# Layer 0's start and layer 1's start: eight conditioning pieces used whole, block 1's input made with block 0's, and the first four score maxima sent from ScalarE's queue

## The chip, the cores and the metric

The kernel runs on one core of a Trainium2 chip. The time is device microseconds (us) of one execution of the whole program; what is compared are medians of several executions. The engines of the core are TensorE (PE in the profile), VectorE (DVE), ScalarE (ACT), GpSimd (POOL) and SyncE (SP); each runs its own instruction list in order and waits on semaphores for the others. Nearly all DMAs are issued by SP.

## What is computed

A two-layer backbone in fp32 on 256 context and 2,048 latent tokens of width 1,024. Cut to what matters here:

```python
def ada_mod(cvec, w, b):                       # conditioning: silu(c) @ ada_w[l] + ada_b[l]
    m = jax.nn.silu(cvec) @ w + b
    shift, scale, gate = jnp.split(m, 3, axis=-1)
def modulate(x, mod, g):
    return rmsnorm(x, g) * (1 + scale) + shift
for l in range(DEPTH):                          # DEPTH = 2
    hp, hs = modulate(xp, mp, ...), modulate(xs, ms, ...)
    # l = 0: one projection of 1,824 columns -> latent attention (8 heads) || pooling, gates, output projection
    # l = 1: one projection -> windowed attention (16 heads, 4 KV heads, |i-j| <= 128, a sink logit per head), gate, output projection
    xp, xs = xp + mp[2] * rmsnorm(op, ...), xs + ms[2] * rmsnorm(os_, ...)
```

## The kernel before

**Precision.** Wide matmuls run on values split into two fp32r parts, high and low: ACT casts the value to fp32r (line 56), and DVE or POOL subtracts that from the value (line 57, the low part). A product is then three matmuls, high by high (line 113), low by high (114) and high by low (115).

**Start of layer 0.** The 2,304 tokens lie in nine blocks of 256 columns (block 0 is the context). The shift and scale of the modulation come from `ada_w` in 16 pieces of 128 x 1,024 values (512 KB), in the order j = 2, 0, 3, 1 of column groups and q = 0 to 3 within each; j = 2 and 0 serve the first four of eight row chunks of `h`, j = 3 and 1 the last four. Each piece is loaded (line 122), split, and multiplied by the conditioning vectors (lines 144, 145, 147). When a group is whole, ACT copies it out (L150), PE transposes it (L153), and DVE adds the bias and the low rows (L155, L156) and makes the scale (L160). `h_stats` loads a block of x, sums squares (ACT L179, POOL L180 to L185, PE L186, then L93 to L100) and multiplies x by the reciprocal root (L190; for block 0 on POOL). `h_mod` makes the high part on ACT (L199), the exact value on DVE (L200) and the low part on DVE (L201), four row chunks at a time. Block 1's `h` is made in the loop over blocks, when block 0 has done its second projection chunk. The projection's chunks 0 to 4 (`cr`, copied out by ACT at L457), the key's rotary part (`wkr`, L473 to L476) and chunks 9 to 12 follow in that order for each block. The weights of chunks 0 to 4 pass through a staging pool of twelve buffers, `ad`; those of `wkr`, chunks 9 to 12, `w_uk`, `w_uv` and `w_uq` through two staging buffers of the pool `p0`, so each load waits until the split of the load two before it is done.

**Start of layer 1.** Attention works in 18 units of 128 queries. Before a unit's scores, `approx1` multiplies its queries by the high part of the keys (L1107, L1115), DVE takes the maxima (L1110, L1116, L1121), and `max_b1` transposes them on PE (L1128), copies them on ACT (L1130) and writes them by DMA into row 64 of the unit's low queries (L1131). The scores' second matmul (L1164) reads that row. Keys lie in a ring that `load_piece` fills (L1043 to L1047). The first two units are looked ahead to during layer 1's last gate block, the following ones while earlier units run.

**Order.** The program is written in one order, and a scheduler orders each engine's list by a simulation of its own; so an edit in one place can move instructions in others. SP's list holds loads and stores alike; a store that waits for its data holds back what stands behind it.

Of the kernel before, what the change touches and what calls it, by code (L numbers as in the profile page):

```python
# [38 lines left out]
def hybrid_step(ctx: ExitStack, tc: tile.TileContext, I, O):  # L39
# [19 lines left out]
    def bank(tag, bufs):  # L59
        return psum.tile([128, 512], F32, tag=tag, name=tag, bufs=bufs)  # L60
# [73 lines left out]

    adaps = {}

    def ada_piece(l, j, q, wh, wl, ep):
        if q == 0:
            adaps[l, j] = bank("M", 3)
        ps = adaps[l, j]  # L140
        for i in range(2):
            k = 2 * q + i
            if k:
                pe.matmul(ps[0:2], lhsT=sch[:, k, 0:2], rhs=wl[:, i], start=False, stop=False)
            pe.matmul(ps[0:4], lhsT=sch[:, k], rhs=wh[:, i], start=k == 0, stop=k == KD - 1)
            if not k:
                pe.matmul(ps[0:2], lhsT=sch[:, k, 0:2], rhs=wl[:, i], start=False, stop=False)
        if q == 3:
            row = ep.tile([4, 512], F32, tag="adarow", name="adarow", bufs=1)
            act.copy(row, ps[0:4])  # L150
            pt = bank("M", 3)[:, 0:16].rearrange("p (m c) -> p m c", m=4)
            for m in range(4):
                pe.transpose(pt[:, m], row[:, 128 * m:128 * m + 128], ident[0:4, 0:4])  # L153
            ms = mods[l][:, 4 * j:4 * j + 4]
            dve.tensor_tensor(out=ms, in0=pt[:, :, 0:2], in1=adab[:, l, 4 * j:4 * j + 4].unsqueeze(2).to_broadcast([128, 4, 2]), op=ALU.add)  # L155
            dve.tensor_tensor(out=ms, in0=pt[:, :, 2:4], in1=ms, op=ALU.add)  # L156
            o = 4 * (j % 2)
            for c in range(2):
                if j in (2, 3):
                    dve.scalar_tensor_tensor(out=amod[l][:, o:o + 4, c], in0=ms[:, :, c], scalar=1.0, in1=npre[l][:, o:o + 4],  # L160
                                             op0=ALU.add, op1=ALU.mult)
                elif j in (4, 5):
                    dve.tensor_tensor(out=gmod[l][:, o:o + 4, c], in0=ms[:, :, c], in1=npost[l][:, o:o + 4], op=ALU.mult)
# [1 line left out]

    r_d = [dram.tile([128, T], F32, name=f"r{l}_d") for l in range(2)]

    def h_stats(hp, b, l, src, again, eng=None):
        cols = slice(256 * b, 256 * b + 256)
        x = hp.tile([128, KD, 256], F32, tag="xb", name="xb", bufs=1)  # L170
        sp.dma_start(out=x, in_=src[:, :, cols])
        if again:
            r = hp.tile([128, 256], F32, tag="rs_y256", name="rs_y", bufs=2)
            sp.dma_start(out=r, in_=r_d[l][:, cols])
        else:
            ss = bank("A", 1)[:, 0:256]
            for i in range(2):
                sq = hp.tile([128, 4, 256], F32, tag="sq", name="sq", bufs=box["sqb"])
                act.activation(out=sq, in_=x[:, 4 * i:4 * i + 4], func=AF.Square)  # L179
                pool.tensor_tensor(out=sq[:, 0:2], in0=sq[:, 0:2], in1=sq[:, 2:4], op=ALU.add)  # L180
                if i == 0:
                    s0 = hp.tile([128, 256], F32, tag="rs_t256", name="s0", bufs=1)
                    pool.tensor_tensor(out=s0, in0=sq[:, 0], in1=sq[:, 1], op=ALU.add)
            for i in range(2):
                pool.tensor_tensor(out=s0, in0=s0, in1=sq[:, i], op=ALU.add)  # L185
            pe.matmul(ss, lhsT=ones, rhs=s0, start=True, stop=True)  # L186
            r = rstd_of(hp, ss, [(0, 256, D)])
            sp.dma_start(out=r_d[l][:, cols], in_=r)
        for c in (slice(0, 4), slice(4, 8)):
            (eng or dve).tensor_tensor(out=x[:, c], in0=x[:, c], in1=r.unsqueeze(1).to_broadcast([128, 4, 256]), op=ALU.mult)  # L190
        return x

    def h_mod(hp, b, l, x):
# [163 lines left out]
    h0 = {}  # L357
    for i, (j, q) in enumerate([(j, q) for j in (2, 0, 3, 1) for q in range(4)]):
        if i == 4:
            h0[0] = h_stats(p0, 0, 0, xT, False, pool)  # L360
        ada_piece(0, j, q, *wload(ad, *wslot(p0, i % 9), ada_src(0, j, q), bufs=12), ad)


    w_in = {}
# [1 line left out]
    def w_in_load(c, s, eng=None, stg=p0, bufs=2):  # L366
        w_in[c] = wload(stg, *wslot(p0, s), W0[c], eng, bufs)

    for c in range(5):
        w_in_load(c, c, (dve, pool)[c % 2], ad, 12)  # L370
    h0[0] = h_mod(p0, 0, 0, h0[0])
    close_ad()
    lr, close_lr = open_pool("lr", "right")

# [73 lines left out]
    for b in range(NBL):  # L448
        h = h0.pop(b)
        t0 = 256 * b  # L450
        cols = slice(t0, t0 + 256)
        CS = None
        raw = lr.tile([128, 5, 256], F32, tag="cr", name="cr", bufs=1)
        for c in range(5):
            if b == 0 and c == 2:
                wkr_load()
            act.copy(raw[:, c], block_mm("S", w_in[c], h))  # L457
            if todo and c:
                todo.pop(0)()
            if c == 1 and b + 1 < NBL:  # L460
                h0[b + 1] = make_h(p0, b + 1, 0, xT)
        while todo:
            todo.pop(0)()
        if b == 2:
            ctx_part()
        if b:
            CS = lr.tile([128, 2, 256], F32, tag="CS", name="CS", bufs=1)
            for i in range(2):
                sp.dma_start(out=CS[:, i], in_=I["rope0"][i][:, t0 - SEQ:t0])
        ps = bank("S", 3)[0:64, 0:256]  # L470
        for k in range(KD):
            if k:
                pe.matmul(ps[0:32], lhsT=wkr[:, k - 1, 0:32], rhs=h[1][:, k - 1], start=False, stop=False)  # L473
            if k == KD - 1:
                pe.matmul(ps[0:32], lhsT=wkr[:, k, 0:32], rhs=h[1][:, k], start=False, stop=False)
            pe.matmul(ps, lhsT=wkr[:, k], rhs=h[0][:, k], start=k == 0, stop=k == KD - 1)  # L476
        e = p0.tile([128, 256], F32, tag="ev", name="ev", bufs=3)[0:32]
        act.copy(e, ps[32:64])
        dve.tensor_tensor(out=e, in0=ps[0:32], in1=e, op=ALU.add)
        if b == 0:  # L480
            sp.dma_start(out=O["state_krope"], in_=e)
        else:
            e = rope(lr, e, CS[0:32, 0], CS[0:32, 1], swap8)
        store_split(lr, e, kr_d, slice(0, 32), slice(kcol(t0), kcol(t0) + 256))
        c_hl = norm(b, raw)
        todo = lr_parts(b, c_hl, CS)
        for c in range(4):
            if b == 0:
                w_in_load(9 + c, 5 + c)
            spill(p0, block_mm("S", w_in[9 + c], h), vp_d[128 * c:128 * c + 128], cols)  # L490
            if b == 0:
                (lambda: lw_load("k", I["w_uk"]), lambda: lw_load("v", I["w_uv"]),
                 lambda: (lw_load("q0", I["w_uq"][0]), lw_load("q1", I["w_uq"][1])), lambda: lw_load("q2", I["w_uq"][2]))[c]()
# [630 lines left out]
    def max_b1(u):  # L1124
        t0 = UN1[u][0]
        mm = mxs.pop(u)
        pt = bank("M", 3)[0:16, 0:128]
        pe.transpose(pt, f(mm), ident)  # L1128
        ms = const.tile([16, 128], F32, tag="bms", name="bms", bufs=2)
        act.copy(ms, pt)  # L1130
        sp.dma_start(out=f(QV[u % NQ][1])[64:65], in_=ms)  # L1131
        es = const.tile([16, 128], F32, tag="bes", name="bes", bufs=2)
        act.activation(out=es, in_=pt, func=AF.Exp, scale=-SWA_SCALE, bias=sinkc)
        sp.dma_start(out=snk_d[:, t0:t0 + 128], in_=es)
# [87 lines left out]
        load_ctx()  # L1222

    def look_ahead(u):
        q1_to(u + 1)
        now1[0] = -22
        look1_to(8 * u + 8)
        max_b1(u)
        events1.clear()


    for b in range(NBL):
        next_h(NBL + b)
        h = h1.pop(NBL + b)
        for i, c in enumerate(range(8) if b < NBL - 1 else (5, 6, 0, 1, 2, 3, 4, 7)):
            if b == 0:
                w1_load(10 + c, c)
            spill(p1, block_mm(None if b < NBL - 1 else "S", w1[10 + c], h), g1_d[128 * c:128 * c + 128], slice(256 * b, 256 * b + 256), True)
            if i == 1 and b + 1 < NBL:
                next_h(NBL + b + 1)  # L1240
            if i == 3 and b + 1 == NBL:
                look_ahead(1)
        if b == 2:
            swa_start()
        if b == NBL - 2:
            ring["VLR"] = h1p.tile([128, 8, 256], F32R, tag="xb", name="VLR", bufs=1)
            load_piece(9)
            look_ahead(0)
    close_p1()
    tc.keep_in_program_order(act.preload_act_table_set("natural_log_exp_and_others"))  # L1250

# [21 lines left out]
    first = {}  # L1273
    for k, (u, g, i) in enumerate(seq1):
        first.setdefault(u, k)
    pace = ([-22] + [first[u] - 5 for u in range(NU1)], [0] + [8 * (u + 1) for u in range(NU1)])
    for p in range(8):
        at1(-21 if p < 3 else first[2 * p - 2] - 15, lambda p=p: load_piece(p))
    for m in range(NPRE):
# [127 lines left out]
```

## Time and profile before

| | |
|---|---|
| median of 3 executions | 3169.73 us (3160.95 to 3170.72) |
| profiled execution | 3158.63 us, span 3156.9 us |
| PE busy | 3008.6 us, 95% of the span |
| DVE, ACT, POOL busy | 70%, 56%, 50% |
| TensorE's mean granted clock | 0.981 of full speed |

The profile is of one execution, 11.1 us shorter than the median. Positions below are microseconds from the start of its span. "L145" is line 145 of the kernel before. A row of a timeline gives start, duration, engine, line, operation, output and inputs, shape and count, and in brackets the engine's idle time just ahead of it and what ended it.

### The profile page before, as it was taken

How to read it: one execution, taken by the hardware profiler on the slowest of the kernel's cores; microseconds unless marked ns; L12 is line 12 of the kernel's file. 1: busy time of each engine (PE TensorE's matmuls, PEld its weight loads, DVE VectorE, ACT ScalarE, POOL GpSimd, SP SyncE). 2: the span in 40 equal slices, each digit the busy share in tenths (PEclk: the TensorE clock that was granted, in tenths of full speed). 3: DMA queues.
4: the chain of work that ended last, by engine and by line, in shares of the span. 5: the costliest groups of instructions: out<-in, count | busy, mean ns of one | idle time of the engine just before them, and what ended most of it. 6: DMA issues, size and time to landing. Idle time of an engine off the chain costs nothing. (4 is left out here: it accounts for less than half of the span.)

```text
span 3156.9 us, 53087 instructions
## 1 busy us (share of the span) xinstructions
PE 3008.6 (95%) x19120; PEld 2587.7 (82%) x19120; DVE 2215.6 (70%) x3992; ACT 1777.0 (56%) x3579; POOL 1584.3 (50%) x1414
## 2 busy tenths in 40 slices
PE   6999999999999999999999999999997999989998
PEld 4999988897777777777679999999996776666998
DVE  6656657977888888888856656677324888767555
ACT  6444444436777777777774433333324877776433
POOL 3223232205777787777774534656002555455553
PEclk8999999999999999999999999999998999999999
DMA  6544468743202202212105554446527344441553
GB/s 237 157 137 133 149 193 257 244 129 90 55 19 56 61 16 58 56 42 65 57 12 177 169 188 150 138 129 190 151 94 153 83 105 102 99 98 50 164 171 118
DMA packets 379681, 375.09 MB, mean 119 GB/s; under 512 B 27904, under 2 KB 344952, under 8 KB 378264
## 3 DMA queue, kind: packets, MB, share of 16 engines
q1 hardware_dynamic: 379404, 371.68, 41.4%
q8 instruction: 150, 2.46, 0.3%
q14 instruction: 115, 0.94, 0.1%
q10 hardware_dynamic: 12, 0.00, 0.0%
HBM read 242.13 MB, written 129.24 MB: 118 GB/s over the span
## 5 line engine op out<-in xcount | busy, mean ns | idle before, releaser
L626 POOL TENSOR_TENSOR acc<-acc,ph 128x512 f32<-128x512 f32 x352 | 458.8, 1303 | 66.7 <-ACT ph L602 42.0
L602 ACT ACTIVATE ph<-S 128x512 fp32r<-128x512 f32 (+1 forms) x592 | 350.9, 593 | 195.1 <-PE S L600 186.9
L553 DVE TENSOR_REDUCE pm<-M 128x1 f32<-128x512 f32 (+1 forms) x656 | 392.1, 625 | 71.9 <-PE M L552 68.0
L614 DVE TENSOR_TENSOR pl<-S,ph 128x512 fp32r<-128x512 f32 (+1 forms) x496 | 334.8, 677 | 63.1 <-ACT S L607 55.4
L113 PE MATMUL S<-hh,wh 128*128 128x256 f32 x1296 | 370.1, 286 | 4.4 <-ACT wh L56 2.8
L114 PE MATMUL S<-hl,wh 128*128 128x256 f32 x1296 | 368.6, 285 | 4.1 <-DVE hl L201 4.1
L115 PE MATMUL S<-hh,wl 128*128 128x256 f32 x1296 | 368.5, 285 | 0.5 <-POOL wl L57 0.5
L607 ACT ACTIVATE S<-S 128x512 f32<-128x512 f32 (+1 forms) x496 | 291.7, 588 | 0.0
L113 PEld LDWEIGHTS S<-hh,wh 128*128 128x128 f32 x1296 | 249.4, 193 | 8.7 <-ACT wh L56 3.3
L114 PEld LDWEIGHTS S<-hl,wh 128*128 128x128 f32 x1296 | 249.7, 193 | 6.4 <-DVE hl L201 4.8
L115 PEld LDWEIGHTS S<-hh,wl 128*128 128x128 f32 x1296 | 249.4, 193 | 2.4 <-POOL wl L57 0.9
L598 PE MATMUL S<-QS,KHL 97*128 97x512 f32 (+1 forms) x592 | 236.6, 400 | 7.6 <-DVE pl L614 7.5
L599 PE MATMUL S<-QS,KHL 96*128 96x512 f32 (+1 forms) x592 | 235.3, 398 | 0.0
L600 PE MATMUL S<-QS,KHL 96*128 96x512 f32 (+1 forms) x592 | 233.0, 394 | 0.0
L552 PE MATMUL M<-KHL,QS 96*128 96x512 f32 (+1 forms) x656 | 227.0, 380 | 6.2 <-DVE pm L553 5.7
L639 PE MATMUL B<-pl,VV 128*65 128x512 f32 (+1 forms) x592 | 228.3, 396 | 1.2 <-DVE pl L614 1.0
L636 PE MATMUL A<-ph,VV 128*128 128x512 f32 (+1 forms) x592 | 215.0, 400 | 0.2 <-ACT ph L602 0.2
L1181 POOL TENSOR_TENSOR bpl<-bpf,bph 128x512 fp32r<-128x512 f32 x136 | 177.0, 1301 | 53.0 <-ACT bpf L1169 40.7
L113 PE MATMUL M<-hh,oh 128*128 128x256 f32 x696 | 197.1, 283 | 3.3 <-ACT oh L56 3.3
L114 PE MATMUL M<-hl,oh 128*128 128x256 f32 x696 | 195.5, 281 | 0.0
L115 PE MATMUL M<-hh,ol 128*128 128x256 f32 x696 | 195.3, 281 | 0.0
L1173 POOL TENSOR_SCALAR_AFFINE_SELECT bpf<-bpf 128x512 f32<-128x512 f32 x120 | 78.6, 655 | 203.8 <-ACT bpf L1169 189.6
(378 smaller groups left out, 9546.8 us busy)
## 6 DMA issues: line engine op xcount, KB each, us to landing
q_d<-ehl SPq DMA_DIRECT2D x126, 256.0 KB
stg<-in_ada_w SPq DMA_DIRECT2D x48, 512.0 KB
xb<-in_xT SPq DMA_DIRECT2D x18, 1024.0 KB
xb<-x_d SPq DMA_DIRECT2D x18, 1024.0 KB
stg<-in_w SPq DMA_DIRECT2D x35, 512.0 KB
hh<-q_d SPq DMA_DIRECT2D x24, 512.0 KB
kn_d<-ehl SPq DMA_DIRECT2D x40, 256.0 KB
v_d<-ve SPq DMA_DIRECT2D x20, 512.0 KB
```

Of the source, the lines that this page charges most:

```text
L113: pe.matmul(ps, lhsT=wh, rhs=xh, start=i == 0, stop=False)
L114: pe.matmul(ps, lhsT=wh, rhs=xl, start=False, stop=False)
L115: pe.matmul(ps, lhsT=wl, rhs=xh, start=False, stop=i == n - 1)
L553: dve.tensor_reduce(out=pms[u][:, s, i:i + 1], in_=ps[:, :w], axis=AX.X, op=ALU.max)
L598: pe.matmul(S[:, :n], lhsT=KH[s][0:97, kc], rhs=qh, start=True, stop=False)
L599: pe.matmul(S[:, :n], lhsT=KH[s][0:96, kc], rhs=ql[0:96], start=False, stop=False)
L600: pe.matmul(S[:, :n], lhsT=KL[s][0:96, kc], rhs=qh[0:96], start=False, stop=True)
L602: act.activation(out=ph[:, :n], in_=S[:, :n], func=AF.Exp, scale=MLA_SCALE)
L607: act.activation(out=pf[:, :n], in_=S[:, :n], func=AF.Exp, scale=MLA_SCALE)
L614: (pool if i in YS else dve).tensor_tensor(out=pl[:, :n], in0=pf[:, :n], in1=f(ph)[:, :n], op=ALU.subtract)
L626: pool.tensor_tensor(out=acc[:, :n], in0=acc[:, :n] if ph0 is None else f(ph0)[:, :n], in1=f(ph)[:, :n], op=ALU.add)
L639: pe.matmul(B[0:65, :n], lhsT=V[:, kts[i], 64:129], rhs=pl[:, :n], start=i == 0, stop=i == nk - 1)
```

## The change

- Pieces 0 to 7 of layer 0's conditioning (j = 2, 0) are handled as before. Pieces 8 to 15 (j = 3, 1) are not split: the fp32 piece goes into two fp32 matmuls with the fp32 conditioning vectors. Their result has two rows instead of four.
- Block 0's x by reciprocal root moves from POOL to DVE. The low parts of the first five projection weights are made by DVE, DVE, POOL, DVE, POOL (before DVE, POOL, DVE, POOL, DVE).
- Block 1's x is loaded ahead of the last two whole pieces, and its `h` is made right behind block 0's, ahead of the loop over blocks. The loop makes the next block's `h` from block 1 on.
- In layer 1 the DMA of the maxima (L1131) is issued by ACT for the first four units and by SP for the others. The look-aheads of units 0 and 1 are written into the last gate block at chunks 1, 2, 4 and 6, and the pacing table that interleaves later look-aheads starts accordingly.

```diff
     def ada_piece(l, j, q, wh, wl, ep, whole=None):
...
+        nr = 4 if whole is None else 2
         for i in range(2):
             k = 2 * q + i
+            if whole is not None:
+                pe.matmul(ps[0:2], lhsT=scf[:, k], rhs=whole[:, i], start=k == 0, stop=k == KD - 1)
+                continue
...
-            (eng or dve).tensor_tensor(out=x[:, c], in0=x[:, c], in1=r.unsqueeze(1).to_broadcast([128, 4, 256]), op=ALU.mult)
+            dve.tensor_tensor(out=x[:, c], in0=x[:, c], in1=r.unsqueeze(1).to_broadcast([128, 4, 256]), op=ALU.mult)
...
-        ada_piece(0, j, q, *wload(ad, *wslot(p0, i % 9), ada_src(0, j, q), bufs=12), ad)
+        if i < 8:
+            ada_piece(0, j, q, *wload(ad, *wslot(p0, 5 + i % 4), ada_src(0, j, q), bufs=12), ad)
+        else:
+            whole = ad.tile([128, 1024], F32, tag="stg", name="stg", bufs=12).rearrange("p (k m) -> p k m", k=2)
+            sp.dma_start(out=whole, in_=ada_src(0, j, q))
+            ada_piece(0, j, q, None, None, ad, whole)
...
-    for c in range(5):
-        w_in_load(c, c, (dve, pool)[c % 2], ad, 12)
+    for c in range(2):
+        w_in_load(c, c, dve, ad, 12)
+    h0[1] = h_stats(ad, 1, 0, xT, False)
     h0[0] = h_mod(p0, 0, 0, h0[0])
+    for c in range(2, 5):
+        w_in_load(c, c, (pool, dve)[c % 2], ad, 12)
+    h0[1] = h_mod(p0, 1, 0, h0[1])
...
-            if c == 1 and b + 1 < NBL:
+            if c == 1 and 0 < b < NBL - 1:
                 h0[b + 1] = make_h(p0, b + 1, 0, xT)
...
-        sp.dma_start(out=f(QV[u % NQ][1])[64:65], in_=ms)
+        (act if u < 4 else sp).dma_start(out=f(QV[u % NQ][1])[64:65], in_=ms)
...
     def look_ahead(u):
-        q1_to(u + 1)
         now1[0] = -22
         look1_to(8 * u + 8)
-        max_b1(u)
         events1.clear()
...
-            if i == 3 and b + 1 == NBL:
-                look_ahead(1)
+            if b + 1 == NBL:
+                {1: lambda: q1_to(2), 2: lambda: look_ahead(0), 4: lambda: (max_b1(0), look_ahead(1)),
+                 6: lambda: max_b1(1)}.get(i, lambda: None)()
...
-            look_ahead(0)
+            q1_to(1)
...
-    pace = ([-22] + [first[u] - 5 for u in range(NU1)], [0] + [8 * (u + 1) for u in range(NU1)])
+    pace = ([-6] + [first[u] - 5 for u in range(2, NU1)], [16] + [8 * (u + 1) for u in range(2, NU1)])
```

In the order that the scheduler makes, three places matter. **PE at the end of the conditioning** (`M` is the bank of a conditioning group or its transposes, `S` one of the projection, `sch` the split and `scf` the fp32 conditioning vectors, `stg` a loaded piece, `A` the bank of the row sums). Before, the last group's matmuls alternate with the first projection matmuls:

```order
L145 MATMUL M<-wh,sch 4x512
L113 MATMUL S<-hh,wh 128x256
L114 MATMUL S<-hl,wh 128x256
L144 MATMUL M<-wl,sch 2x512
L145 MATMUL M<-wh,sch 4x512
L144 MATMUL M<-wl,sch 2x512
L145 MATMUL M<-wh,sch 4x512
L113 MATMUL S<-hh,wh 128x256
L114 MATMUL S<-hl,wh 128x256
```

Now:

```order
L146 MATMUL M<-stg,scf 2x512 x8
L158 MATMUL M<-ident,adarow 128x2 x4
L146 MATMUL M<-stg,scf 2x512 x8
L192 MATMUL A<-s_305,ones 128x256
L113 MATMUL S<-hh,wh 128x256
L114 MATMUL S<-hl,wh 128x256
L115 MATMUL S<-hh,wl 128x256
```

Both whole groups and block 1's row sum stand ahead of the first projection matmul; the last group's transposes follow 14 projection matmuls later, and the matmuls of block 0's four later row chunks after those, in either kernel.

**DVE at block 0's later row chunks** (`wkr`, `kl`, `vl` and `wl` are low parts of weights). Before:

```order
L57 TENSOR_TENSOR wkr<-stg,wkr 128x8x32
L57 TENSOR_TENSOR kl<-stg,kh 128x1024
L200 TENSOR_SCALAR xb<-xb,amod_78,mod_76 128x256 x4
L201 TENSOR_TENSOR hl<-xb,hh 128x1024
L57 TENSOR_TENSOR wl<-stg,wh 128x1024
L57 TENSOR_TENSOR vl<-stg,vh 128x1024
```

Now:

```order
L100 SCALAR_TENSOR_TENSOR rs_y<-rs_t,rs_y 128x256
L207 TENSOR_TENSOR hl<-xb,hh 128x1024
L196 TENSOR_TENSOR xb<-xb,rs_y 128x1024 x2
L206 TENSOR_SCALAR xb<-xb,amod_78,mod_76 128x256 x4
L207 TENSOR_TENSOR hl<-xb,hh 128x1024
L206 TENSOR_SCALAR xb<-xb,amod_78,mod_76 128x256 x4
L207 TENSOR_TENSOR hl<-xb,hh 128x1024
L57 TENSOR_TENSOR wkr<-stg,wkr 128x8x32
L57 TENSOR_TENSOR kl<-stg,kh 128x1024
```

All of block 1's `h` stands between block 0's last low part and the split of `wkr`, which stood ahead of block 0's last low part before.

**ACT at the maxima of layer 1's third unit** (`bo` is an attention output, `bms` the maxima, `bes` the sink's term, `bph` the high part of the probabilities). Before:

```order
L1199 COPY bo<-A 65x512
L1199 COPY bo<-B 65x512
L1130 COPY bms<-M 16x128
L1133 ACTIVATE bes<-M,sinkc 16x128
L1167 ACTIVATE bph<-S 128x512
```

Now:

```order
L1214 COPY bo<-A 65x512
L1214 COPY bo<-B 65x512
L1145 COPY bms<-M 16x128
L1148 ACTIVATE bes<-M,sinkc 16x128
L1146 DMA hl<-bms 1x16x128
L1182 ACTIVATE bph<-S 128x512
```

The DMA has come to ACT's list two instructions behind the copy; in SP's list it stood behind two loads of KAR, a store and a load of KBR. PE's list from the first look-ahead matmul to the end of the third unit's scores is the same in both kernels, and the SP and PE lists of units 4 to 17 differ in the places of stores and look-aheads.

## Rows read from the trace of the kernel before

**Rows 1.** The page: the span, and its first part (busy time, share of the span, instructions by engine).

```profile
span 3156.9 us, 53087 instructions
PE 3008.6 (95%) x19120; PEld 2587.7 (82%) x19120; DVE 2215.6 (70%) x3992; ACT 1777.0 (56%) x3579; POOL 1584.3 (50%) x1414
```

**Rows 2.** Windows of the start: length, then busy time (and count) of each engine, granted clock, share of the 16 DMA engines, GB/s.

```profile
20.00:30.00 10.00, 7.23 (x28) 2.28 (x27) 9.74 (x12) 7.24 (x10) 3.73 (x3) 0.83 1.05 385
30.00:40.00 10.00, 4.69 (x21) 1.67 (x18) 9.90 (x15) 7.21 (x11) 7.02 (x3) 0.85 0.79 309
```

**Rows 3.** PE's timeline of the start: transposes of the second group, the waits, the last `wkr` matmul, and the first wait for block 1's `h`.

```profile
27.19 0.41 PE L153 MATMUL M<-ident,adarow 4*128 4x4 f32 x4 [1.62 <-ACT adarow L150]
...
38.61 0.58 PE L113 MATMUL S<-hh,wh 128*128 128x256 f32 x1 [2.77 <-ACT wh L56]
...
43.09 0.59 PE L144 MATMUL M<-wl,sch 128*2 128x512 f32 x1 [2.71 <-DVE wl L57]
...
56.32 0.58 PE L114 MATMUL S<-hl,wh 128*128 128x256 f32 x1 [2.69 <-DVE hl L201]
...
69.86 0.28 PE L476 MATMUL S<-hh,wkr 128*64 128x256 f32 x1
...
84.99 0.39 PE L114 MATMUL S<-hl,wh 128*128 128x256 f32 x1 [0.85 <-DVE hl L201]
```

**Rows 4.** PE's timeline: two neighbouring fp32r matmuls of 512 columns in the conditioning; and a row sum, which is an fp32 matmul of 256 columns (two records), with the fp32r matmuls of 256 columns behind it.

```profile
28.45 0.39 PE L144 MATMUL M<-wl,sch 128*2 128x512 f32 x1
28.68 0.40 PE L145 MATMUL M<-wh,sch 128*4 128x512 f32 x1
...
134.44 0.59 PE L186 MATMUL A<-s,ones 128*128 128x256 f32 x2
134.69 0.47 PE L113 MATMUL S<-hh,wh 128*128 128x256 f32 x1
134.99 0.28 PE L114 MATMUL S<-hl,wh 128*128 128x256 f32 x1
```

**Rows 5.** DVE's timeline: low parts of two pieces, exact values and a low part of `h`, two of a reciprocal root's steps, and x by reciprocal root (two instructions); and one such instruction on POOL.

```profile
30.17 4.53 DVE L57 TENSOR_TENSOR wl<-stg,wh 128x1024 fp32r<-128x1024 f32 x2
...
37.11 1.37 DVE L200 TENSOR_SCALAR xb<-xb,amod,mod 128x256 f32<-128x256 f32 x4
...
55.04 1.23 DVE L201 TENSOR_TENSOR hl<-xb,hh 128x1024 fp32r<-128x1024 f32 x1
...
77.33 0.43 DVE L98 SCALAR_TENSOR_TENSOR rs_t<-rs_y 128x256 f32<-128x256 f32 x1
...
78.25 0.87 DVE L100 SCALAR_TENSOR_TENSOR rs_y<-rs_t,rs_y 128x256 f32<-128x256 f32 x1
79.15 2.36 DVE L190 TENSOR_TENSOR xb<-xb,rs_y 128x1024 f32<-128x1024 f32 x2
...
30.34 3.28 POOL L190 TENSOR_TENSOR xb<-xb,rs_y 128x1024 f32<-128x1024 f32 x1 [6.45 <-DVE rs_y L100]
```

**Rows 6.** The way of chunk 10's and chunk 12's weights through the two staging buffers: their loads on SP, the cast of chunk 12's on ACT, and their low parts on DVE, between them the low part of `q0`, which frees chunk 12's buffer.

```profile
52.11 0.33 SPq L122 DMA_DIRECT2D stg<-in_w  x1
...
56.92 1.23 DVE L57 TENSOR_TENSOR wl<-stg,wh 128x1024 fp32r<-128x1024 f32 x1 [0.65 <-ACT wh L56]
...
66.65 1.49 DVE L57 TENSOR_TENSOR q0l<-stg,q0h 128x768 fp32r<-128x768 f32 x1
...
68.17 0.33 SPq L122 DMA_DIRECT2D stg<-in_w  x1
...
72.50 1.05 ACT L56 CAST wh<-stg 128x1024 fp32r<-128x1024 f32 x1 [0.21 <-DMA stg<-in_w]
...
73.58 1.43 DVE L57 TENSOR_TENSOR wl<-stg,wh 128x1024 fp32r<-128x1024 f32 x1 [1.35 <-ACT wh L56]
```

**Rows 7.** PE's timeline at the start of layer 1's attention: the last look-ahead matmul ahead of the third unit's scores, and those scores.

```profile
2432.12 0.57 PE L1107 MATMUL M<-KAR,hh 128*128 128x384 f32 x1
2440.90 1.22 PE L1164 MATMUL S<-hl,KBR 96*128 96x512 f32 x2 [8.22 <-DMA hl<-bms]
```

**Rows 8.** SP's timeline at the same place.

```profile
2431.13 0.79 SPq L1043 DMA_DIRECT2D KAR<-k_d  x1
...
2433.31 0.94 SPq L1045 DMA_DIRECT2D KBR<-k_d  x1
2434.36 0.62 SPq L1131 DMA_DIRECT2D hl<-bms  x1
```

**Rows 9.** ACT's timeline there: the maxima's copy and the sink's term.

```profile
2428.00 0.26 ACT L1130 COPY bms<-M 16x128 f32<-16x128 f32 x1 [0.44 <-PE M L1128]
2428.17 0.35 ACT L1133 ACTIVATE bes<-M,sinkc 16x128 f32<-16x128 f32 x1
```

**Rows 10.** Windows around it, columns as in rows 2.

```profile
2425.00:2450.00 25.00, 15.25 (x55) 11.11 (x54) 13.96 (x42) 6.97 (x14) 4.71 (x5) 0.66 0.74 151
2450.00:2475.00 25.00, 25.00 (x122) 18.62 (x121) 18.24 (x49) 20.69 (x41) 14.58 (x14) 1.00 0.41 87
```

**Rows 11.** The page's third part: DMA queues, with packets, MB and share of 16 engines.

```profile
q1 hardware_dynamic: 379404, 371.68, 41.4%
...
q10 hardware_dynamic: 12, 0.00, 0.0%
```

**Rows 12.** A query of line 571, where layer 0's attention issues its first two units' maxima from ACT (duration min/median/max in ns, then first and last start).

```profile
L571 ACTq DMA_DIRECT2D QS<-ms x2: 608/896/1184, 706.1 to 707.4; - x2
```

More of the change, by code (lines that the diff above doesn't have):

```diff
@@ L135, in hybrid_step, with ada_piece @@
     adaps = {}
-    def ada_piece(l, j, q, wh, wl, ep):
+    def ada_piece(l, j, q, wh, wl, ep, whole=None):
         if q == 0:
@@ L148, in ada_piece @@
         if q == 3:
-            row = ep.tile([4, 512], F32, tag="adarow", name="adarow", bufs=1)
-            act.copy(row, ps[0:4])
-            pt = bank("M", 3)[:, 0:16].rearrange("p (m c) -> p m c", m=4)
+            row = ep.tile([4, 512], F32, tag="adarow", name="adarow", bufs=1)[0:nr]
+            act.copy(row, ps[0:nr])
+            pt = bank("M", 3)[:, 0:4 * nr].rearrange("p (m c) -> p m c", m=4)
             for m in range(4):
-                pe.transpose(pt[:, m], row[:, 128 * m:128 * m + 128], ident[0:4, 0:4])
+                pe.transpose(pt[:, m], row[:, 128 * m:128 * m + 128], ident[0:nr, 0:nr])
             ms = mods[l][:, 4 * j:4 * j + 4]
             dve.tensor_tensor(out=ms, in0=pt[:, :, 0:2], in1=adab[:, l, 4 * j:4 * j + 4].unsqueeze(2).to_broadcast([128, 4, 2]), op=ALU.add)
-            dve.tensor_tensor(out=ms, in0=pt[:, :, 2:4], in1=ms, op=ALU.add)
+            if nr == 4:
+                dve.tensor_tensor(out=ms, in0=pt[:, :, 2:4], in1=ms, op=ALU.add)
             o = 4 * (j % 2)
@@ L166, in hybrid_step, with h_stats @@
     r_d = [dram.tile([128, T], F32, name=f"r{l}_d") for l in range(2)]
-    def h_stats(hp, b, l, src, again, eng=None):
+    def h_stats(hp, b, l, src, again):
         cols = slice(256 * b, 256 * b + 256)
@@ L359, in hybrid_step @@
         if i == 4:
-            h0[0] = h_stats(p0, 0, 0, xT, False, pool)
-        ada_piece(0, j, q, *wload(ad, *wslot(p0, i % 9), ada_src(0, j, q), bufs=12), ad)
+            h0[0] = h_stats(p0, 0, 0, xT, False)
+        if i < 8:
[4 more added lines that the diff above has]
+            ada_piece(0, j, q, None, None, ad, whole)
     w_in = {}
```

## The prediction

> **What bounds the kernel now.** I read the page first: PE is busy 3,008.6 of 3,156.9 us [rows 1]. At most 148 us can be had without removing PE work, and an edit that shortens work on another engine counts only where PE waits for it. So I looked for PE's waits at the two places of the change.
>
> At the start, DVE is the bound from 20 to 40 us: it is busy 9.74 and 9.90 of each 10 us, while PE has 7.23 and 4.69 [rows 2]. PE waits four times there: for a copy at 27.2, for a cast at 38.6, for a low part of a piece at 43.1, and for block 0's second low part, which lets it go at 56.32 [rows 3]. From there it runs with short waits; one is 0.85 us at 85 for block 1's `h` [rows 3]. The DMA engines are full from 20 to 30 us at 385 GB/s [rows 2]: a 512 KB piece takes 1.36 us.
>
> At the start of layer 1's attention PE ends its look-ahead at about 2432.7 and waits 8.22 us for the third unit's maxima [rows 7]. They were ready for the DMA at 2428.5, behind the copy and the sink's term on ACT [rows 9], but SP issued it at 2434.36, behind the stores and the loads of KAR and KBR in its list [rows 8].
>
> **Whole pieces.** Eight casts, eight low parts and 32 matmuls go. A low part is 1.23 us [rows 6], or 2.3 while POOL multiplies x [rows 5], so DVE is rid of some 10 to 18 us before 48 us. In their place stand 16 fp32 matmuls of 512 columns. The trace has fp32 matmuls of 256 columns: from 134.44 to 134.99, less 0.12 for the fp32r matmul between, is 0.43 us, 3.6 times the fp32r one [rows 4]. For 512 columns I take twice that, 0.86 us. A piece then costs PE 1.72 us, where four fp32r matmuls at 0.23 [rows 4] cost 0.92, and this is more than the 1.36 us of its load: in this stretch PE becomes the bound in DVE's place.
>
> PE is free at 27.5, after the second group's transposes [rows 3]. Group j = 3: 8 x 0.86 = 6.9, to 34.4. Copy and transposes, some 1.1 (0.41 [rows 3] and the copy ahead), to 35.5. Group j = 1: to 42.4. Its last piece, with block 1's 1 MB ahead of it, lands at about 35 by the pace of the queue, so loads hide. Then the row sum 0.43 and 14 first-half projection matmuls at 0.12, and the transposes: 44.9. From there DVE's list (the second place of the order) is: the bias 0.2, a low part 1.23, the three steps of block 1's root 0.43 + 0.43 + 0.87, four exact values 1.37, and the low part 1.23 [rows 5, 6]; 5.8, so block 0's second half is ready at 50.6. Before it was 56.3 [rows 5]: **5.7 us earlier**. x by reciprocal root on DVE, 2.36 for two against 3.28 for one on POOL [rows 5], is ahead of this, where DVE now has time, and costs nothing.
>
> **Block 1's h made early.** It puts 2.36 + 2 x 1.37 + 2 x 1.23 = 7.6 us of DVE work [rows 5] between block 0's last low part and the split of `wkr`: that split ends at 50.6 + 7.6 + 0.4 = 58.6. PE has 34 second-half matmuls and two more projection chunks to do until about 62, so it does not wait for `wkr` itself. What is queued behind it does: the two staging buffers. Chunk 10's load needs the buffer of `wkr`, and from issue to the end of the low part it took 52.11 to 58.15, 6.0 us [rows 6]. So chunk 10 is ready at 64.6, chunk 11 at 70.6. In the other buffer `w_uk` is split at 59.8, `w_uv` at 65.8 and `q0` at 71.5; chunk 12's load starts then, and its cast ended 5.4 us after the issue [rows 6]: 76.9. Before, chunk 12 was ready at 75.0 [rows 6] and PE came to it only at about 80.5 (69.86 + 0.2 [rows 3], three chunks of 24 x 0.12, 1.8 for three row sums at 0.43 and a short wait). So of 5.7 us **3.6 are left** at chunk 12, and 2.1 turn into a wait for its weights. The 0.85 us at 85 go [rows 3], since block 1's `h` is long ready. The start's term is **-4.5 us**: bounds 0, if each of the four loads in the chain takes 1 us longer, and -6.6, if none of it binds (5.7 + 0.85).
>
> **The maxima from ACT's queue.** ACT issues the DMA at 2428.5 instead of SP at 2434.36 [rows 8, 9]; the issue takes ACT 0.6 to 1.2 us by the two such DMAs of layer 0 [rows 12], and ACT has nothing to do there until PE's scores come. When does it land? PE resumed 6.5 us after SP's issue [rows 7, 8], with three key loads ahead in the queue. The page counts ACT's DMAs as a queue of their own: q10 has 12 packets against q1's 379,404 [rows 11]. If that queue does not stand behind the key loads, which are issued later anyway (2431.13 on [rows 8]), the row lands before 2432.7 and the wait goes: **-8.2 us**. If it takes 6.5 us all the same, it lands at 2435.0 and 2.3 us of wait stay: -5.9. I take -8.2, since what the DMA stood behind was issued after 2431. Above that, the granted clock is 0.66 in the window with the wait and 1.00 in the next [rows 10]; without the wait some of the work at half clock may be done at full: up to 2 us more.
>
> A rule speaks against it: the Trainium skill, "DMA: Bandwidth & Descriptors", section "Issuing engines are not separate DMA queues", says that DMAs of all issuing engines run on the same 16 DMA engines and interleave, and that several issuers save only the time of issuing. By it the term would be the 5.9 us of issue alone. The rows agree with its first half (one set of 16 engines, full in the start), and no row here shows a landing of q10 beside a full q1.
>
> **The look-aheads spread out.** PE's list is the same from the first look-ahead to the end of the third unit's scores, so this moves nothing there: 0. In later units stores and look-aheads change places in SP's and PE's lists; the trace has no row for that, and I bound it by the waits of this place, half of 8.2 each way: -4 to +4, taken as 0.
>
> **Sum.** -4.5 - 8.2 = -12.7 us. The profiled execution took 3,158.6 with a span of 3,156.9: it would be 3,145.9. The median of the runs is 3,169.7, 11.1 above it; with the same difference the forecast is **3,157.0 us**.
>
> **Rivals.**
> - *The DMA lands late all the same*, 6.5 us after its issue. For it: the 16 engines are busy 0.74 of that window [rows 10]. Against: the separate queue and the later key loads. Term -5.9, total -10.4: 3,159.3. Chance 0.13. (The rule of the Trainium skill above would give this case.)
> - *The start gives nothing*: the chain of two staging buffers takes 1 us more per load, or PE runs the fp32 matmuls at half clock, where 16 of them take 27.5 us instead of 13.8 (the granted clock was 0.83 and 0.85 with PE half idle [rows 2]; now PE is full, which speaks against). In the first case the term is 0, total -8.2: 3,161.5; in the second block 0 is ready at 64.4, 8 us later than before, and the total is about 0: 3,169. Chance 0.2 and 0.04.
> - *Slower*: from the fifth unit on the maxima still go by SP. If a moved store, which waits for ACT's copy, stands ahead of them or of a unit's queries, PE waits there as it did for the third unit, 8.2 us each time [rows 7]. One such wait leaves -4.5, two are +3.7 (3,173), and from the second on the change loses. For it: SP's list is not the same in units 4 to 17. Against: stores stood ahead of the later maxima before too, and the trace has no second wait of that size for them. Chance 0.07.
> - *It does more*: nothing binds in the chain and the clock adds 2 us: -16.8, 3,152.9. Chance 0.1.
>
> **How the numbers follow.** The forecast has 0.46. A measurement of this kernel can tell about 0.3%, 9.5 us, from no change. The forecast, the late landing and the larger gain lie beyond that bound or at it, the empty start within it; with the +-4 us of the later units I get 0.56 faster, 0.36 the same, 0.08 slower. The range runs from the larger gain with 4 us of later units and some spread of the runs (3,146) to the case of an empty start with 8 us on top (3,169).
>
> **What would show it.** In the changed kernel's trace: the fp32 matmuls back to back from about 27 to 42 us with DVE no longer full; PE released for block 0's second half near 50.6; a wait of about 2 us near 75 on a cast of chunk 12's weights; no wait on block 1's `h`; a wait below 2 us ahead of the third unit's scores. The forecast is wrong if the fp32 matmuls cost over 1 us each, if PE waits over 5 us for weights between 60 and 80, if the maxima's wait stays, or if a wait over 4 us appears in units 4 to 17.

## The result

| | before | after |
|---|---|---|
| median of 6 executions each | 3166.09 us | 3182.34 us (3176.38 to 3190.6) |
| ratio | 1 | 1.0055 [1.0037, 1.0073] |
| profiled execution, span | 3156.9 us [rows 1] | 3174.6 us |

The changed kernel is slower by 0.55%, some 16 to 17 us, outside the predicted range. Two marks on PE cut both profiled executions into three stretches: the third unit's first scores, and the first output projection that waits for its weights. (Units are numbered from 0 below: the third unit is unit 2.)

| stretch | before | after | difference |
|---|---|---|---|
| start to third unit's scores | 2440.90 [rows 7] | 2439.87 | -1.0 |
| to the output projection | 498.84 | 523.45 | **+24.6** |
| to the end of the span | 217.2 | 211.3 | -5.9 |
| sum | 3156.9 | 3174.6 | +17.7 |

The ends of the second stretch are the first rows below; it will be called the **middle stretch**. It repeats well: 498.2 to 500.3 in seven kernels, the one before and six of those below (`layer1_only`, `whole_only`, `after_keep`, `before_keep`, `start_keep`, `whole_keep`). The other two move by several us between executions of equal work (the last is 211 to 217 in all profiles, and from the row at 183 below to the third unit's scores it is 2,251 to 2,266), so only the middle one is read to the microsecond. Within this spread the first stretch shows only 1.0 us of the 7.3 that the start (4.25) and the third unit's shorter wait (3.1) gained. The third unit's wait is 5.14 us now (8.22 [rows 7]). PE's timeline of the changed kernel, and the projection's row of the kernel before behind it:

```profile
2439.87 1.22 PE L1179 MATMUL S<-hl,KBR 96*128 96x512 f32 x2 [5.14 <-DMA hl<-bms]
...
2963.32 0.57 PE L113 MATMUL M<-hh,oh 128*128 128x256 f32 x1 [3.75 <-ACT oh L56]
```

```profile
2939.74 0.58 PE L113 MATMUL M<-hh,oh 128*128 128x256 f32 x1 [3.34 <-ACT oh L56]
```

**The start** came out near what was worked out (how much of that is luck is said further down). PE's timeline of the changed kernel:

```profile
26.59 7.03 PE L146 MATMUL M<-stg,scf 128*2 128x512 f32 x16
34.33 0.41 PE L158 MATMUL M<-ident,adarow 2*128 2x2 f32 x4 [0.72 <-ACT adarow L155]
34.67 7.03 PE L146 MATMUL M<-stg,scf 128*2 128x512 f32 x16
...
52.16 0.58 PE L114 MATMUL S<-hl,wh 128*128 128x256 f32 x1 [4.65 <-DVE hl L207]
...
72.49 0.70 PE L410 MATMUL B<-sq,ones 128*128 128x256 f32 x2 [2.01 <-POOL sq L106]
...
79.35 0.39 PE L113 MATMUL S<-hh,wh 128*128 128x256 f32 x1 [2.09 <-ACT wh L56]
...
183.03 0.63 PE L113 MATMUL M<-ch,kh 128*128 128x256 f32 x3 [2.06 <-ACT ch L56]
```

Each group's eight fp32 matmuls (two records each) take 7.03 us back to back. Block 0's second half goes on at 52.16 (56.32 [rows 3]), chunk 12 waits 2.09 us for its cast, and no wait for block 1's `h` is left. The row at 183.03 stands in the kernel before at 187.28. In windows, DVE is no longer full, and PE nearly is from 30 us on (before: [rows 2]):

```profile
20.00:30.00 10.00, 7.79 (x26) 2.10 (x25) 7.06 (x10) 2.48 (x6) 3.70 (x3) 0.95 1.06 374
30.00:40.00 10.00, 9.28 (x26) 2.02 (x25) 6.51 (x13) 6.73 (x9) 6.25 (x5) 1.00 1.04 402
```

**The middle stretch.** PE's waits from 2455 to 2950 us, first of the kernel before, then of the changed one (engine, bank, line, what is waited for: us in total, times, longest):

```profile
PE M L1107 <- DMA mix0h<-q_d: 6.6, 3, 2.7
PE A L1195 <- DVE bpl L1181: 4.1, 8, 1.0
PE M L1107 <- DMA hh<-q_d: 4.0, 3, 2.2
PE B L1195 <- DVE bpl L1181: 3.5, 6, 0.7
...
PE A L1195 <- POOL bpl L1181: 1.4, 1, 1.4
...
PE B L1195 <- POOL bpl L1181: 0.4, 1, 0.4
```

```profile
PE M L1122 <- DMA hh<-q_d: 12.9, 7, 2.9
PE B L1210 <- DVE bpl L1196: 7.4, 12, 0.9
PE M L1122 <- DMA mix0h<-q_d: 5.8, 3, 3.0
PE A L1210 <- DVE bpl L1196: 2.2, 5, 0.8
PE A L1210 <- POOL bpl L1196: 1.9, 1, 1.9
...
PE B L1210 <- POOL bpl L1196: 1.1, 2, 0.9
```

`q_d` holds the queries (`hh` and `mix0h` are buffers for their high part), `bpl` is the low part of the probabilities. The look-aheads meet queries that have not landed ten times, 18.7 us in all, where it was six times and 10.6. One of them, with SP's row of the load and PE's of the wait, in the changed kernel:

```profile
2554.09 0.60 SPq L1100 DMA_DIRECT2D hh<-q_d  x1
...
2562.86 0.58 PE L1122 MATMUL M<-KAR,hh 128*128 128x384 f32 x2 [2.91 <-DMA hh<-q_d]
```

There are three query buffers, so unit u's load is issued when unit u-3 has done its scores. The load landed 8.8 us after its issue; PE came to the look-ahead after 5.9. How far a look-ahead stands behind that point is in PE's list, which the scheduler makes. Counted in score steps (a step is the score matmuls of one unit, one group of heads and one tile of keys; 328 in all; 499 us over 328 is 1.5 us each), for units 6 to 17:

```
before       17 14 10  5  5  6  6  4  2  3  3  4
after        10  5  4  2  5  3  4  2  3  2  4  3
```

8.8 us are six steps: eleven of the changed kernel's twelve look-aheads stand below that (ten wait), seven of the kernel before's (six wait); unit 8, with 4 steps, is the wait in the rows above. The text says below how much of the 24.6 us this accounts for.

### The profile page after: what moved, and what is told of

Read it like the earlier page. It is cut to its first block, busy times and chain, and to the rows that moved or that the text cites. A ratio compares the mean times of both kernels' runs of the same rounds, so it can differ in the third digit from the quotient of the medians.

```text
span 3174.6 us, 53061 instructions
## 1 busy us (share of the span) xinstructions
PE 3017.9 (95%) x19120; PEld 2586.4 (81%) x19120; DVE 2202.6 (69%) x3984; ACT 1769.5 (56%) x3571; POOL 1577.0 (50%) x1412
## 3 DMA queue, kind: packets, MB, share of 16 engines
q1 hardware_dynamic: 379276, 371.65, 41.2%
```

## The experiments

The theories. **A**: the edit of the start shifts the scheduler's simulated times; that moves the later look-aheads ahead of their queries, and the middle stretch gets longer. **B**: the loss is of layer 1's own edits (ACT's queue, spreading). **C**: the query waits only replace others; the loss is elsewhere. For the third unit's maxima, **D**: they land late behind the loads, whatever queue issues them; **E**: SP's issue time sets the wait.

### The start alone, layer 1 alone

`start_only` is the changed kernel with layer 1's three edits taken back; `layer1_only` has these and the start of before.

```diff
-        (act if u < 4 else sp).dma_start(out=f(QV[u % NQ][1])[64:65], in_=ms)
+        sp.dma_start(out=f(QV[u % NQ][1])[64:65], in_=ms)
...
-    pace = ([-6] + [first[u] - 5 for u in range(2, NU1)], [16] + [8 * (u + 1) for u in range(2, NU1)])
+    pace = ([-22] + [first[u] - 5 for u in range(NU1)], [0] + [8 * (u + 1) for u in range(NU1)])
```

> The whole edit of the start, with layer 1's code as before. Theory A (the start's edit shifts the scheduler's simulated times, and by that the places of layer 1's look-aheads in PE's list: unit 7's maxima stand 20 score steps ahead of its first score instead of 10, so that PE meets the look-ahead while the queries are still being loaded): the loss stays, about 1.005 of before or a little more, about 17 to 22 us slower, with some 19 us of PE waits for query loads in units 4 to 17 (before 10.6). Theory B (layer 1's own edits, the DMA from ACT's queue and the pacing, cost it): the start's 5 us are kept, 0.998 of before.

> The edits of layer 1 alone (DMA of the first four maxima from ACT, look-aheads spread out, pacing), with the start as before. Theory A: PE's list in layer 1 is that of before, so only the third unit's wait changes, from 8.2 to about 5 us: 3 us faster, 0.999. Theory B: 15 to 20 us slower, 1.005 to 1.006.

`start_only`: 1.0041 [1.0026, 1.0056], 3176.99 us, some 13 us slower where A expected 17 to 22. Its look-aheads stand as in the changed kernel, its middle stretch is 517.6 us, and its query waits are the same (18.6 us):

```profile
PE M L1122 <- DMA hh<-q_d: 13.0, 7, 2.8
...
PE M L1122 <- DMA mix0h<-q_d: 5.7, 3, 3.0
```

`layer1_only`: 0.9992 [0.9979, 1.0005], 3160.01 us; the look-aheads of units 4 to 17 stand as before, middle stretch 500.3, third unit's wait 5.7. Its query waits are longer than those of the kernel before (12.3 us, six times), at no cost to the stretch:

```profile
PE M L1107 <- DMA mix0h<-q_d: 6.7, 3, 2.5
PE M L1107 <- DMA hh<-q_d: 5.6, 3, 2.4
```

So 18.8 of the 24.6 us come with the start's edit, 2,400 us ahead of where they are paid. Layer 1's edits alone bring 1.4. B falls as the main cause; the 5.8 us between `start_only` and the changed kernel, with the same look-aheads and query waits in both, are not explained.

### The two halves of the start's edit

`whole_only`: whole pieces, but block 1's `h` in the loop as before. `early_h_only`: all 16 pieces split, block 1's `h` early. Layer 1 as before in both.

```diff
-    h0[1] = h_stats(ad, 1, 0, xT, False)
...
-    h0[1] = h_mod(p0, 1, 0, h0[1])
...
-            if c == 1 and 0 < b < NBL - 1:
+            if c == 1 and b + 1 < NBL:
```

```diff
-        if i < 8:
-            ada_piece(0, j, q, *wload(ad, *wslot(p0, 5 + i % 4), ada_src(0, j, q), bufs=12), ad)
-        else:
...
+        ada_piece(0, j, q, *wload(ad, *wslot(p0, i % 9), ada_src(0, j, q), bufs=12), ad)
```

> The start with whole pieces 8 to 15, x by reciprocal root on DVE and the new split of the weights' low parts, but block 1's h made in the loop over blocks as before; layer 1's code as before. Theory A: here the look-aheads of units 5 to 8 stand only 4 steps ahead of their units, the query loads have long landed, and layer 1's attention is not slower than before; with 2 to 5 us from the start about 0.997 to 0.999 of before. Theory B has no layer-1 edit to blame here either and gives the start's gain alone, 0.998 to 0.999; it differs from A in the waits for query loads, which by B stay at 10.6 us.

> Block 1's h made with block 0's, with all 16 pieces split as before (x by reciprocal root on DVE); layer 1's code as before. Theory A: the look-aheads stand nearly where they do in the changed kernel, so layer 1 loses 12 to 20 us of it again; the start itself does not gain, since DVE gets more work where it is full: 1.005 to 1.008 of before. Theory B: only the start's loss, 1 to 5 us, 1.000 to 1.0015.

`whole_only`: 1.0004 [0.9991, 1.0018], 3167.43 us: not the small gain that A gave it, though the middle stretch is 499.6 and the query waits 6.5 us. Where that gain went is not shown. `early_h_only`: 1.0077 [1.0057, 1.0097], 3192.16 us, middle stretch 520.1; DVE stays full there (10.00 of 10 us from 30 to 40) and PE waits 5.21 us at 41.04 and 4.85 at 60.43. The lists, as above:

```
whole_only   16 16 16 16 15 12 14 10  5  2  3  3
early_h_only 10  5  2  4  5  2  5  2  3  2  4  3
```

The order is not a matter of more or less work at the start: with one half most look-aheads stand further behind than before, with the other as close as with both. That the start's edit reaches the order through the scheduler's simulated times, as A says, is argued; the runs show the edit and the order.

### The order held

One line per look-ahead keeps its first matmul where the program writes it, from unit 3 on. `after_keep` is the changed kernel with it, `before_keep` the kernel before.

```diff
-                    pe.matmul(ps[:, b:b + w], lhsT=qa[:, h], rhs=KAR[:, g, a:a + w], start=x == 0, stop=x == len(runs) - 1)
+                    mmi = pe.matmul(ps[:, b:b + w], lhsT=qa[:, h], rhs=KAR[:, g, a:a + w], start=x == 0, stop=x == len(runs) - 1)
+                    if u >= 3 and hp == 0 and g == 0 and h == h0 and x == 0:
+                        tc.keep_in_program_order(mmi)
```

> The changed kernel with one thing added: the first look-ahead matmul of each unit from the fourth on is kept at its place in the written order, so that no unit's look-ahead starts more than 21 score steps ahead of the unit's first score (in the changed kernel up to 36). Theory A (the look-aheads ran into the query loads): the waits for query loads in units 4 to 17 fall from 18.7 to under 4 us, layer 1 loses nothing any more, and the time is 12 to 20 us below the changed kernel's, about 0.998 to 1.000 of before. Theory C (in that order it is not the queries: PE waits for DVE, ACT and POOL there, or the clock falls for other reasons): the query waits move to others, and the time stays at 1.004 to 1.006.

> The kernel before with the same hold on the look-aheads. Theory A: its 10.6 us of waits for query loads fall to under 4, 4 to 8 us faster than before, 0.997 to 0.999. Theory C: no change or slower, since PE has less to fill its other waits with, 1.000 to 1.002.

Both have 19 steps for each of the units 6 to 17, and no wait for queries. `after_keep`: **0.9983 [0.9974, 0.9992]**, 3157.23 us, middle stretch 500.3; that is some 23 us below the changed kernel, where A expected 12 to 20. `before_keep`: 0.9995 [0.9982, 1.0008], 3162.95 us, middle stretch 499.6. PE's waits in the stretch, `after_keep`, then `before_keep`:

```profile
PE A L1212 <- DVE bpl L1198: 10.3, 18, 1.4
...
PE B L1212 <- DVE bpl L1198: 2.5, 7, 0.7
```

```profile
PE A L1197 <- DVE bpl L1183: 11.5, 18, 2.4
PE A L1195 <- ACT bph L1181: 4.1, 2, 3.5
...
PE B L1197 <- DVE bpl L1183: 2.0, 4, 0.7
```

The same edit takes 23 us out of the middle stretch of one kernel and leaves the other as it was. A forecast 4 to 8 us for `before_keep`; they didn't come: its 10.6 us of query waits were replaced by waits for the probabilities' low part on DVE (13.5 us, before 7.6) and for their high part on ACT (4.1, before none). That much of C holds: removing query waits is not worth their sum.

### The loss made in the kernel before

`before_far` is `before_keep` with the look-aheads paced to be done 21 steps ahead of a unit's scores, not 5; `after_near` is `after_keep` with 2 steps. Paced earlier, a look-ahead stands closer behind its queries' load.

```diff
-    pace = ([-22] + [first[u] - 5 for u in range(NU1)], [0] + [8 * (u + 1) for u in range(NU1)])
+    pace = ([-22] + [first[u] - (5 if u < 4 else 21) for u in range(NU1)], [0] + [8 * (u + 1) for u in range(NU1)])
```

```diff
-    pace = ([-6] + [first[u] - 5 for u in range(2, NU1)], [16] + [8 * (u + 1) for u in range(2, NU1)])
+    pace = ([-6] + [first[u] - (5 if u < 4 else 2) for u in range(2, NU1)], [16] + [8 * (u + 1) for u in range(2, NU1)])
```

> The kernel before, nothing of the change in it, with the look-aheads paced 16 score steps earlier from the fifth unit on and their first matmuls held there. That gives PE the list that the changed kernel has: units 6 to 9 have their maxima at score steps 57, 72, 89 and 112 (changed kernel 62, 77, 92, 112; before 69, 86, 102, 117). Theory A: this order alone makes the loss, 12 to 20 us slower than before, 1.004 to 1.006, with 17 to 20 us of waits for query loads in units 4 to 17. If the loss needs anything else of the change (the start's loads, ACT's queue), it is 1.000 to 1.001.

> after_keep with the look-aheads paced 3 steps later still (they start 18 steps ahead of their unit's first score instead of 21, and the maxima are done 3 steps ahead instead of 5). Theory A has nothing to gain there, since no query is waited for any more; if the maxima now come too late, their DMA is waited for in more units: 0 to 6 us slower than after_keep.

```
before_far    5  3  4  3  5  3  4  3  4  5  3  4
after_near   22 22 22 22 22 22 22 22 22 22 23 23
```

`before_far`: 1.0083 [1.0063, 1.0103], 3194.6 us, middle stretch 523.9, as in the changed kernel, with nothing changed at the start; the whole loses more than the 1.004 to 1.006 expected. Its query waits:

```profile
PE M L1107 <- DMA hh<-q_d: 11.2, 7, 2.6
PE M L1107 <- DMA mix0h<-q_d: 10.3, 4, 3.5
```

`after_near`: 1.002 [1.0009, 1.0032], 3169.61 us, middle stretch 507.6, some 12 us slower than `after_keep` where at most 6 were expected. Too late costs as well: now the scores wait for maxima.

```profile
PE S L1181 <- DMA hl<-bms: 5.4, 2, 4.2
```

### What the parts are worth in a good order

`start_keep` and `whole_keep` are `start_only` and `whole_only` with the held order (the edit of `after_keep`).

> The start's edit with layer 1's code as before and the hold on the look-aheads: after_keep without the DMA from ACT's queue and without the spreading. The third unit's wait should be 8.2 to 8.5 us instead of 4.9: 2 to 4 us slower than after_keep, about 0.999 to 0.9995 of before. If the queue is worth nothing in the end (what PE gains there it waits for DVE a little later), it equals after_keep, 0.998.

> As start_keep, but block 1's h is made in the loop over blocks as before; so the start's gain is that of the whole pieces alone. If the early h is worth its 0.85 us and no more, this equals start_keep within 1 us; by the prediction's chain (the early h holds back the staging buffers and costs 2.1 us of wait at chunk 12) it is 1 to 2 us faster than start_keep.

`start_keep`: 0.9981 [0.9969, 0.9993], 3159.49 us. I had expected it 2 to 4 us slower than `after_keep`, for want of ACT's queue; it is equal within the intervals, so **the queue and the spreading are worth nothing that can be measured** (each interval is 3 to 4 us wide either way), though the third unit's wait is 8.3 us here and 4.9 in `after_keep`. `whole_keep`: 0.9984 [0.9973, 0.9995], 3161.25 us; against `start_keep`, the early `h` cannot be told from nothing either. That it is 2 parts in a thousand below `whole_only`, with a middle stretch only 1.4 us shorter (498.2), is not explained. Against `before_keep` the start's edit gives 1.4 parts in a thousand, 4.4 us; the intervals of the two overlap.

### The maxima without the large loads ahead of them

In `after_keep_hold` and `before_keep_hold` the loads of unit 4's queries and of the fourth piece of keys wait for the third unit's maxima: ACT first writes the maxima into the buffers that these loads fill. They are `after_keep` and `before_keep` otherwise.

```diff
+        if u == 4:
+            for z in (qa[0:16, 0], qa[64:80, 0], qb[0:16, 0]):
+                act.copy(z, ms2[0])
...
+        if p == 3:
+            for z in (KAR[0:16, 0, a:a + 128], KAR[64:80, 0, a:a + 128], KBR[0:16, 0, a:a + 128]):
+                act.copy(z, ms2[0])
```

> The changed kernel with both holds, so the maxima go by ACT's queue with nothing ahead on the DMA engines. By D the wait is under 2 us as with SP's queue, and the queue makes no difference (the changed kernel's 5.1 us with ACT's queue was the same landing time behind the same loads). With the start's 5 us kept this is the best of the four, about 0.996 of before, 3,150 to 3,155 us. By E the changed kernel's wait would have fallen to under 2 already, so E cannot explain its 5.1 us.

> As before_keep, and the loads of unit 4's queries and of the fourth key piece wait until the third unit's maxima are copied (six small copies on ACT out of the maxima into the places that these loads overwrite, which cost ACT 1.5 us where it idles). The maxima's DMA stays on SP. Theory D (the maxima land late because some 1.5 MB of queries and keys stand ahead of them on the 16 DMA engines, whatever queue they go by): the third unit's wait falls from 8.2 to under 2 us, 5 to 7 us faster than before_keep. Theory E (it is SP's issue time): SP issues the maxima at once here too, so E gives the same; it differs from D in the next run.

First the changed kernel without the hold, ACT's and SP's rows:

```profile
2427.47 0.57 SPq L1100 DMA_DIRECT2D mix0h<-q_d  x1
...
2428.85 2.09 SPq L1102 DMA_DIRECT2D mix0l<-q_d  x1
...
2430.48 0.35 ACT L1148 ACTIVATE bes<-M,sinkc 16x128 f32<-16x128 f32 x1
2433.73 0.52 ACTq L1146 DMA_DIRECT2D hl<-bms  x1
```

The maxima are ready at 2430.8, but ACT issues the DMA at 2433.73: in its list the DMA waits for a completion counter that a DMA eight places earlier counts too, by that order unit 4's first query load. PE goes on at 2439.87, 6.1 us after the issue. With the hold:

```profile
2435.22 0.55 ACTq L1155 DMA_DIRECT2D hl<-bms  x1
...
2437.46 0.80 PE L1190 MATMUL S<-hl,KBR 96*128 96x512 f32 x1 [0.75 <-DMA hl<-bms]
...
2452.13 0.19 DVE L1236 TENSOR_TENSOR rsum<-rsum 128x32 f32<-128x32 f32 x1 [6.26 <-DMA rsum<-o_d]
...
2452.97 0.45 PE L1221 MATMUL B<-bpl,VAR 128*65 128x512 f32 x1 [4.08 <-DVE bpl L1207]
```

2.2 us from issue to PE, and a wait of 0.75, with no query or key load ahead. D holds for ACT's queue: what makes the row late after its issue is what is loaded beside it. But the held loads come later, a small load behind them keeps DVE until 2452.13, and PE waits 4.08 us there: middle stretch 510.7, 0.9991 [0.998, 1.0003], 3161.82 us, not the best of the four at 0.996 that was expected. By SP, `before_keep_hold` has 4.2 us left in that wait (SP issued at 2440.63, 2.3 us after the maxima were copied, behind other entries of its list, as E has it; PE went on 3.4 us later) and a second one of 3.5: 1.0013 [1.0002, 1.0025], 3167.34 us, middle stretch 507.9, and not the 5 to 7 us gain on `before_keep` that was expected. Each theory has the part of the wait that its queue leaves: E before the issue, D after it.

## Why the prediction was wrong

**The step that failed** is "The look-aheads spread out": "in later units stores and look-aheads change places ...; bounded -4 to +4, taken as 0". That term was 24.6 us in the middle stretch. Three things were wrong in it. The cause was in the main not the spreading, but the start's edit (`start_only`), for whose effect on later lists the sum had no term. And the bound came from a wait of another kind: half of the third unit's single wait, instead of the slack of each look-ahead against its own queries. The rows for that were there: the query waits of the kernel before (10.6 us, six times), the time from a load's issue to its landing, and the two lists, which showed the changed positions. And PE's list is not the same to the end of the third unit's scores: it parts at 2442.07 in the changed kernel, a few steps into them, with a look-ahead matmul where the kernel before goes on with the probabilities, and PE waits there:

```profile
2447.46 0.50 PE L1130 MATMUL M<-KC,hh 128*128 128x256 f32 x2 [2.13 <-DVE bmx L1131]
```

**What makes up the 24.6 us:** query waits +8.1 (10.6 to 18.7); waits for probabilities' low parts +3.2 by the rows above (9.4 with 1.8 on POOL, to 12.6 with 3.0 on POOL); the new wait of 2.1 at 2447.46, in unit 3's look-ahead. All of PE's waits in the stretch (those over 0.15 us) come to 26.9 us before and 41.2 now, so 0.9 is left for the others. The rest has no wait of its own. Some of it is the granted clock, in a window the mean of its two levels (2.4 and 1.2 GHz): over the eight windows from 2500 to 2900 the share below 1.00 comes to 11.5 us in the changed kernel, 5 in the one before. In `before_far`, which loses as much, it is only 6. Two of these windows, changed kernel, then the first of them in `after_keep` (0.93 there in the kernel before too):

```profile
2700.00:2750.00 50.00, 45.10 (x197) 31.97 (x197) 35.44 (x86) 35.11 (x68) 21.81 (x23) 0.93 0.39 85
2750.00:2800.00 50.00, 41.81 (x174) 27.63 (x173) 31.77 (x67) 32.87 (x64) 27.10 (x26) 0.93 0.59 142
```

```profile
2700.00:2750.00 50.00, 49.35 (x234) 36.33 (x234) 39.70 (x99) 40.09 (x79) 26.07 (x28) 1.00 0.55 111
```

That is 8.1 + 3.2 + 2.1 + 0.9 + 6.5 = 20.8 of 24.6, if all of the clock's share is lost time; 4 us are not assigned. That the order is the cause doesn't rest on this sum, but on `before_far` and `after_keep`. That it works through the query waits is in part argued. Up to 12.3 us of them only take the place of others: all of PE's waits are 27 to 29 us in the seven kernels with a stretch of 498 to 500, and 38 to 44 in the four with 17 to 22 us of query waits. Waits are not all, though: `after_near` has 28 us of them and a stretch of 507.6. No run leaves the look-aheads where they are and has the queries there in time, with a fourth query buffer for instance.

**Mis-sized: the maxima**, -8.2 in the sum. The wait fell by 3.1, since the reason for taking the upper end ("what the DMA stood behind was issued after 2431") overlooked unit 4's query loads, issued from 2427.47 (2425.05 in the kernel before). Besides, ACT issued the row only 2.9 us after it was ready. The rival "the DMA lands late all the same", 6.5 us after issue, was right on the landing (6.1) and missed the later issue. The Trainium skill, "DMA: Bandwidth & Descriptors", section "Issuing engines are not separate DMA queues", says that DMAs of every issuing engine share the 16 DMA engines and interleave; the trace agrees, with 6.1 us beside the loads and 2.2 without them. And even a short wait was worth nothing that can be measured in the end (`start_keep`, `after_keep_hold`).

**Right in size, in part by luck: the start**, -4.5. The row at 183.03 was at 187.28, 4.25 us earlier. Single executions lie up to 4 us apart there; over the six profiles with the changed start the mean is 184.1, over the five with the start of before 188.3, so 4.2. By steps: an fp32 matmul took 0.88 us (0.86). Block 0's second half came at 52.16 (50.6), since a low part on DVE took 2.30 us where 1.23 was taken, and the four exact values 3.26 where 1.37 was taken, both partly beside low parts on POOL:

```profile
44.55 2.30 DVE L57 TENSOR_TENSOR wl<-stg,wh 128x1024 fp32r<-128x1024 f32 x1
...
47.12 0.72 DVE L206 TENSOR_SCALAR xb<-xb,amod,mod 128x256 f32<-128x256 f32 x2
...
48.09 2.54 DVE L206 TENSOR_SCALAR xb<-xb,amod,mod 128x256 f32<-128x256 f32 x2
```

The wait of 2.01 us on POOL at 72.49 was not foreseen. Chunk 12's wait is 2.09 (2.1), but PE came to it at 77.26 where 74.8 follows from the prediction (80.5 less 5.7), and the cast let it go at 79.35 (76.9): both 2.4 us late, so the wait fits by luck. In the kernel before, chunk 12 starts here:

```profile
80.97 0.28 PE L113 MATMUL S<-hh,wh 128*128 128x256 f32 x1
```

So 1.6 us of gain were left at chunk 12, not 3.6; the rest came between there and 183, 0.85 of it at the wait for block 1's `h` that is gone, the remainder by no term of the sum. That block 1's `h` adds to the gain as a whole is not shown. The prediction also says that PE waits four times at the start; two more waits of over 1 us stand in that trace (1.22 at 34.76, 1.66 at 53.01), and no term rests on it.

**The rivals.** "The start gives nothing" fell: the granted clock was 0.95 and 1.00 in the two windows with the fp32 matmuls, so they did not run at half clock. "It does more" fell too. "Slower" (0.07) had the right stretch and the wrong mechanism: not stores ahead of the queries in SP's list with waits of 8.2 us, but ten waits of at most 3.0. So "a wait over 4 us in units 4 to 17", named as a sign of being wrong, never appeared. "The maxima's wait stays" did: 5.14 us, with below 2 forecast.

## What to carry to other kernels

Where a scheduler orders the lists, an edit can be paid for far from its place: compare the lists over the whole program, and for every prefetched use work out the steps between the point where its buffer comes free and its first use, against the time of the load in the trace. Hold that distance by a stated order, and then price the edit itself. A wait is worth removing only as far as the next engine is ahead: in this kernel the query waits of the kernel before were replaced by waits on DVE and ACT, and the third unit's wait, with the loads held, by one on DVE.

## What the runs showed of the hardware

- A row of 8 KB reached its reader 6.1 us after issue beside the query loads, and 2.2 us after with no query or key load ahead, from the same engine's queue.
- ACT held a DMA whose data was ready for 2.9 us; its list has a wait for a shared completion counter there. That the counter is the reason was read from the list and not tried by itself.
- DVE's low part of 1,024 columns took 2.30 us from 44.55 on, while POOL made one until 45.78 (2.39 us, from 43.39), and 1.23 by itself [rows 6]. Two exact values took 2.54 us from 48.09 on, while POOL made one from 47.83 to 50.17, and 0.72 just ahead of that.
- Waits of 0.9 to 3.0 us, ten of them, went with TensorE's granted clock at 0.93 to 0.97 in five of the eight windows from 2500 to 2900; eleven in `before_far` with 0.97 in four.
